# State space preparation of a hybrid trunk: the small response products of two quads issued together, their results side by side in the scratch

## The chip, the cores and the metric

The kernel runs on one core of a Trainium2 chip. The metric is the device time of one execution in microseconds (us). Before the change it is 2791.68 us, the median of 3 runs (2790.18 to 2793.75). One execution was also taken by the hardware profiler; its own time and its trace are what the sections below read.

## The reference

The program is a decoder trunk of two layers over 256 tokens with width 2048. Each layer is a token mixer, a cross-attention to 256 memory positions and a squared-ReLU MLP, each behind an RMSNorm, with residual adds. Layer 0 mixes tokens with a chunked gMLP, layer 1 with a state space layer (S5). All is float32. The change touches only what prepares layer 1's state space layer. Its reference is, cut to what matters:

```python
def s5_glu(h, w_in, lam_re, lam_im, log_dt, bm_re, bm_im, cm_re, cm_im, d_skip, w_out, b_out):
    u = (h @ w_in).reshape(bsz, seq, 128, 16)             # 128 channel groups of 16
    lam_bar = jnp.exp(lam * dt)                            # 128 x 64 complex poles
    b_bar = ((lam_bar - 1.0) / lam)[..., None] * bmat      # 128 x 64 x 16
    bu = jnp.einsum('gpc,bsgc->sbgp', b_bar, u)
    states[s] = lam_bar * states[s - 1] + bu[s]            # an associative scan over positions
    y = jnp.einsum('gcp,sbgp->bsgc', cmat, states).real + d_skip * u
    val, gate = jnp.split(gelu(y) @ w_out + b_out, 2, axis=-1)
    return val * jax.nn.sigmoid(gate)
```

The kernel cuts the 256 positions into 32 chunks of T = 8. Inside a chunk, y is a causal convolution: the response at distance w is the real 16 x 16 matrix C lam_bar^w B_bar of each group, for w = 0 to 7, and D is added at w = 0. These matrices depend on parameters alone. Computing them is the work that the change edits.

## The kernel before, in words

**Weight streams.** Nearly the whole kernel is a stream of matrix products with weights read once. A load of 512 KB (`wraw`, issued by SyncE at L123, four buffers) is split into a high part by ScalarE (`whi`, L102) and a rest by VectorE (`wlo`, L103), three buffers of each. A split load is called a weight tile here. TensorE then runs 12 or 16 matmuls on it: high part by activation high and low part, and rest by activation high part. In the MLP, up-projection tiles are lines L167 (512 wide) and L172 (256 wide), down-projection tiles are L806, L807 and L809 (512 wide). The MLP's hidden activations pass from the accumulator over ScalarE (`r`, L183), VectorE (L184, L641) and a split of their own (`hh` L102, `hl` L103).

**The preparation.** `ssm_prep` appends small steps to a list of side work. It is worked off during layer 0's MLP: `tick` is called after each weight tile, and at every second call one step is recorded at lower priority (a lag of 200). A scheduler of the framework then fixes the order of each engine's instructions at build time; on the chip each engine runs its own list in that order and waits by semaphores.

The 128 groups are treated in 32 quads of four. For each quad q there are three steps:

- `quad(q)` builds `bb`, the B_bar of four groups (L1069 to L1071, VectorE, 128 x 64). There are two `bb` buffers, used in turn; each group's 16 columns are padded to 32 with zeros.
- `quad_q(q)` builds `qt`, the C lam_bar^w (L1079 to L1081, VectorE, 128 x 576 each, two buffers), sends it to the DRAM scratch `Qd`, then multiplies: four matmuls (L1092), one for each group, 32 stationary columns, 128 moving columns, each to its own 32 partitions of one PSUM tile `kp`. In the trace each of these is two instructions, and stands under the tile name `ps`. The responses go from PSUM to `kd`: zeros in the first 7 of 15 blocks (POOL memset, L1095), w = 1 to 7 by a ScalarE copy (L1096), w = 0 with D by VectorE (L1097). Four transfers (L1100, GpSimd queue) write `kd` to the scratch `Kd`, 240 runs of 64 bytes each.
- `quad_p(q)` builds and sends `Pd` (L1110 to L1114).

**The use.** `s5` reads the scratch back on the GpSimd queue (L1144: `pq`, `dq`, `qq`). `own` (L1207) and `outputs` (L1255, L1261) multiply with it in groups of small matmuls; L1207 and L1255 have the same form as L1092, 32 stationary and 128 moving columns, the one 64 and the other 16 instructions in a row.

## Time and profile before

| | |
|---|---|
| median of 3 runs | 2791.68 us (2790.18 to 2793.75) |
| the profiled execution, its own time | 2790.06 us |
| its span, first to last instruction | 2788.4 us |
| TensorE matmul busy | 2765.7 us, 99% |
| VectorE, ScalarE, GpSimd busy | 1986.2, 1395.3, 236.0 us |
| granted TensorE clock, mean | 0.999 |
| the 32 groups of response products (L1092) | 256 instructions, from 779.3 to 1321.5 us |

PE is TensorE's matmuls, PEld its weight loads, DVE VectorE, ACT ScalarE, POOL GpSimd, SP SyncE. Matmuls are pipelined: the recorded duration of one (390 ns for 512 columns) overlaps the next, so what one costs in a stream is the distance from its start to the next start. A row of the timeline gives start, length, engine, line, tiles, shape and count, and in brackets the idle time of the engine ahead of it.

### The profile page before, as it was taken

What the parts mean: (1) busy time and instruction counts of PE and PEld (TensorE: products, weight loads), DVE (VectorE), ACT (ScalarE), POOL (GpSimd) and SP (SyncE); (2) the same over time, 40 slices, a digit from 0 to 9 for tenths busy, and PEclk for the clock granted to TensorE, in tenths of its full rate; (3) what the DMA queues carried; (4) which work ended last, traced back from release to release, by engine and by line L of the source; (5) the groups of instructions that cost most, each with busy time, mean ns of one, the idle gap of its engine ahead of it and who ended that gap; (6) DMA issues with size and microseconds to landing.
All of it is one profiled execution on the core that took longest, in us unless ns stands there. A gap on an engine that the chain in (4) does not pass through costs nothing. (4 is left out here: it accounts for less than half of the span.)

```text
span 2788.4 us, 39687 instructions
## 1 busy us (share of the span) xinstructions
PE 2765.7 (99%) x15020; PEld 2331.1 (84%) x15020; DVE 1986.2 (71%) x2747; ACT 1395.3 (50%) x1801; POOL 236.0 (8%) x434
## 2 busy tenths in 40 slices
PE   9999999999999999999999999999999999999998
PEld 7888888888888888888887888888888888888886
DVE  6765756778978878787568657557777767677665
ACT  6545545555534444444555445445555545455454
POOL 0100000001022222231213100000000000000000
PEclk9999999999999999999999999999999999999999
DMA  8766655547688888887879767564556566565655
GB/s 294 226 216 216 204 177 179 177 156 250 212 261 258 258 257 259 259 257 224 244 244 266 218 199 238 173 196 159 177 156 219 168 217 198 166 218 171 218 180 156
DMA packets 196048, 593.76 MB, mean 213 GB/s; under 512 B 44960, under 2 KB 47184, under 8 KB 195344
## 3 DMA queue, kind: packets, MB, share of 16 engines
q1 hardware_dynamic: 151968, 532.22, 60.6%
q0 software_dynamic: 43744, 58.95, 7.7%
q8 instruction: 117, 1.92, 0.3%
q14 instruction: 75, 0.61, 0.1%
q10 hardware_dynamic: 144, 0.07, 0.0%
HBM read 567.51 MB, written 23.46 MB: 212 GB/s over the span
## 5 line engine op out<-in xcount | busy, mean ns | idle before, releaser
L103 DVE TENSOR_TENSOR wlo<-wraw,whi 128x1024 fp32r<-128x1024 f32 x892 | 1085.1, 1222 | 490.0 <-ACT whi L102 484.3
L102 ACT CAST whi<-wraw 128x1024 fp32r<-128x1024 f32 x892 | 936.9, 1052 | 853.5 <-PE acc L723 202.8
L167 PE MATMUL acc<-act,whi 128*128 128x512 f32 x3072 | 742.3, 391 | 0.9 <-ACT whi L102 0.9
L167 PEld LDWEIGHTS acc<-act,whi 128*128 128x128 f32 x3072 | 562.8, 188 | 111.7 <-issue 2.6
L172 PEld LDWEIGHTS acc<-act,wlo 128*128 128x128 f32 x3072 | 394.9, 191 | 17.6 <-DVE wlo L103 1.9
L172 PE MATMUL acc<-act,wlo 128*128 128x256 f32 x3072 | 403.6, 283 | 1.4 <-DVE wlo L103 1.0
L152 PE MATMUL acc<-whi,act 128*128 128x512 f32 x1472 | 369.7, 393 | 7.1 <-ACT whi L102 6.3
L152 PEld LDWEIGHTS acc<-whi,act 128*128 128x128 f32 x1472 | 274.9, 189 | 64.9 <-ACT whi L102 6.3
L723 PE MATMUL acc<-whi,act 128*128 128x512 f32 x864 | 232.9, 392 | 0.0
L807 PE MATMUL acc<-whi,hl 128*128 128x512 f32 x544 | 213.3, 392 | 0.0
L806 PE MATMUL acc<-whi,hh 128*128 128x512 f32 x544 | 212.7, 391 | 0.0
L152 PE MATMUL acc<-wlo,act 128*128 128x512 f32 x736 | 197.1, 389 | 0.0
L723 PEld LDWEIGHTS acc<-whi,act 128*128 128x128 f32 x864 | 160.4, 188 | 36.5 <-ACT ends L755 1.9
L152 PEld LDWEIGHTS acc<-wlo,act 128*128 128x128 f32 x736 | 138.2, 188 | 28.9 <-DVE wlo L103 0.2
L723 PE MATMUL acc<-whi,hh 128*128 128x512 f32 x378 | 148.4, 393 | 0.0
L723 PE MATMUL acc<-whi,hl 128*128 128x512 f32 x378 | 147.2, 390 | 0.0
L809 PE MATMUL acc<-wlo,hh 128*128 128x512 f32 x544 | 145.9, 390 | 0.0
L723 PE MATMUL acc<-wlo,act 128*128 128x512 f32 x432 | 133.1, 390 | 0.0
L807 PEld LDWEIGHTS acc<-whi,hl 128*128 128x128 f32 x544 | 102.1, 188 | 23.0 <-issue 2.2
L183 ACT COPY r<-acc 128x512 f32<-128x512 f32 x64 | 37.7, 588 | 166.6 <-PE acc L167 166.6
L809 PEld LDWEIGHTS acc<-wlo,hh 128*128 128x128 f32 x544 | 102.1, 188 | 21.5 <-issue 0.2
L806 PEld LDWEIGHTS acc<-whi,hh 128*128 128x128 f32 x544 | 102.1, 188 | 21.4 <-issue 0.4
(365 smaller groups left out, 2763.7 us busy)
## 6 DMA issues: line engine op xcount, KB each, us to landing
wraw<-in_f_w_up SPq DMA_DIRECT2D x256, 512.0 KB, 4.6
wraw<-in_f_w_down SPq DMA_DIRECT2D x228, 512.0 KB, 4.6
wraw<-in_a_w_in SPq DMA_DIRECT2D x64, 512.0 KB, 4.7
wraw<-in_x_w_q SPq DMA_DIRECT2D x64, 512.0 KB, 3.9
wraw<-in_x_w_k SPq DMA_DIRECT2D x64, 512.0 KB, 4.6
wraw<-in_b_w_out SPq DMA_DIRECT2D x64, 512.0 KB, 4.4
wraw<-in_x_w_v SPq DMA_DIRECT2D x48, 512.0 KB, 3.9
wraw<-in_x_w_o SPq DMA_DIRECT2D x48, 512.0 KB, 4.3
```

What stands on the lines that cost most here:

```text
L102: self.nc.scalar.copy(out=hi, in_=src)
L103: return self.nc.vector.tensor_tensor(out=lo, in0=src, in1=hi.bitcast(F32), op=ALU.subtract).ins
L152: nc.tensor.matmul(out[t], a[:, kt, sl], b[:, kk, :], start=st and a is ah, stop=en)
L167: nc.tensor.matmul(acc[:, f, :], hi[:, kk, sl], both[:, kt].rearrange("p a s -> p (a s)"), start=first and kk == 0, stop=last and kk == FK ...
L172: nc.tensor.matmul(acc[:, f, 0:S], lo[:, kk, sl], ah[:, kt, :], start=False, stop=last and kk == FK - 1, skip_group_check=True)
L183: nc.scalar.copy(out=dst, in_=acc[:, :, S:])
L723: mm = lambda s, m, e: nc.tensor.matmul(out, s, m, start=key not in begun, stop=e, skip_group_check=True)
L806: nc.tensor.matmul(acc[:, t, :], ah, hi[:, kk, :], start=kt == 0, stop=False)
L807: nc.tensor.matmul(acc[:, t, :], al, hi[:, kk, :], start=False, stop=False)
L809: nc.tensor.matmul(acc[:, t, :], hid[kt // 4][0][:, kt % 4, sl], lo[:, kk, :], start=False, stop=kt == KT - 1)
```

## The change

The products of two quads (2m and 2m + 1, a pair) are issued together, at the end of the odd quad's `quad_q`, by a new function `products(m)`: eight matmuls into one PSUM tile. One ScalarE copy of twice the size moves w = 1 to 7 of both, and two VectorE instructions add D. `kd` holds both quads side by side in one buffer instead of two; its zeros are written once, in `poles`. Four transfers a pair write it, 240 runs of 128 bytes each, where eight wrote runs of 64 bytes. The scratch's order of axes changes with it, and with that the order in which `outputs` reads `dq`.

```diff
-        self.Kd = mk("Kd", [16, NL, 2, 4, 16])
+        self.Kd = mk("Kd", [16, NL, 4, 2, 16])
...
+            e["kd"] = pool.tile([P, NL, 2, 16], F32, name="kd", bufs=1)
+            nc.gpsimd.memset(e["kd"][:, 0:T - 1], 0.0)
...
             nc.gpsimd.dma_start(out=self.Qd[q // 2][q % 2].rearrange("p r n -> r p n"), in_=qt[:, 1:])
-            kp = self.ps([P, T, 16])
-            for g in range(4):
-                with self.tc.high_priority(offset=g):
-                    nc.tensor.matmul(kp[32 * g:32 * g + 32], bb[:, g], qt[:, 0:T, g, :], start=True, stop=True,
-                                     skip_group_check=True)
-            kd = pool.tile([P, NL, 16], F32, name="kd", bufs=2)
-            nc.gpsimd.memset(kd[:, 0:T - 1, :], 0.0)
-            nc.scalar.copy(out=kd[:, T:, :], in_=kp[:, 1:, :])
-            v.scalar_tensor_tensor(out=kd[:, T - 1, :], in0=eye, scalar=dsk[:, q:q + 1], in1=kp[:, 0, :],
-                                   op0=ALU.mult, op1=ALU.add)
+            e["qt", q] = qt
+            if q % 2:
+                products(q // 2)
+
+        def products(m):
+
+            kp = self.ps([P, 2, T, 16])
+            for i in range(2):
+                bb, qt = e["bb"][i], e.pop(("qt", 2 * m + i))
+                for g in range(4):
+                    with self.tc.high_priority(offset=4 * i + g):
+                        nc.tensor.matmul(kp[32 * g:32 * g + 32, i], bb[:, g], qt[:, 0:T, g, :], start=True, stop=True,
+                                         skip_group_check=True)
+            kd = e["kd"]
+            nc.scalar.copy(out=kd[:, T:].rearrange("p w i c -> p i w c"), in_=kp[:, :, 1:, :])
+            for i in range(2):
+                q = 2 * m + i
+                v.scalar_tensor_tensor(out=kd[:, T - 1, i, :], in0=eye, scalar=dsk[:, q:q + 1], in1=kp[:, i, 0, :],
+                                       op0=ALU.mult, op1=ALU.add)
             for t in range(4):
-                nc.gpsimd.dma_start(out=self.Kd[q // 2][:, :, q % 2, t], in_=kd[32 * t:32 * t + 16])
+                nc.gpsimd.dma_start(out=self.Kd[m][:, :, t], in_=kd[32 * t:32 * t + 16])
...
-                    dq = ahead.pop(("dq", n, i)).rearrange("p (j l t c) -> p l t j c", j=T, l=2, t=4)
+                    dq = ahead.pop(("dq", n, i)).rearrange("p (j t l c) -> p l t j c", j=T, l=2, t=4)
```

Line numbers grow by two from `quad` on and by eleven behind `products`; the products are L1102 in the new file, the copy L1106, the addition of D L1108, the transfers L1111.

The order of instructions changes at two places that matter below. The first is TensorE's list in the up-projection of layer 0's MLP, where the products of the fifth and sixth quad stand (`bb_5745` and `bb_5746` are the two `bb` buffers). Before:

```order
L167 MATMUL acc<-act,whi 128x512 x2
L1092 MATMUL ps<-qt,bb_5745 32x128 x4
L167 MATMUL acc<-act,whi 128x512 x14
L172 MATMUL acc<-act,wlo 128x256 x16
L167 MATMUL acc<-act,whi 128x512 x16
L172 MATMUL acc<-act,wlo 128x256 x16
L167 MATMUL acc<-act,whi 128x512 x8
L1092 MATMUL ps<-qt,bb_5746 32x128 x4
L167 MATMUL acc<-act,whi 128x512 x8
```

The same stretch of TensorE's list in the change:

```order
L172 MATMUL acc<-act,wlo 128x256 x16
L167 MATMUL acc<-act,whi 128x512 x16
L172 MATMUL acc<-act,wlo 128x256 x16
L167 MATMUL acc<-act,whi 128x512 x8
L1102 MATMUL ps<-qt,bb_5745 32x128 x4
L1102 MATMUL ps<-qt,bb_5746 32x128 x4
L167 MATMUL acc<-act,whi 128x512 x8
```

The even quad's four matmuls left their place and stand directly ahead of the odd quad's, which stay where they were. All 32 quads do the same: 16 places instead of 32. TensorE's list is otherwise the same from end to end.

The second is VectorE's list behind the products of the fourth quad (the second of a pair). Before, it reads, from the addition of D to the next rest of a weight tile:

```order
L1097 SCALAR_TENSOR_TENSOR kd<-eye,dsk,ps 128x16
L1069 TENSOR_TENSOR bb_5746<-F,bcq 128x4x16
L1079 TENSOR_TENSOR qt<-T_5684,bcq 128x4x9x16
L1071 TENSOR_TENSOR bb_5746<-bb_5746,tq 128x4x16
L1062 TENSOR_SCALAR bcq<-bcq,sg 128x128
L1080 TENSOR_TENSOR tq<-T_5685,bcq 128x576
L1081 TENSOR_TENSOR qt<-qt,tq 128x4x9x16
L1111 TENSOR_TENSOR tq<-lb 128x512
L103 TENSOR_TENSOR wlo<-wraw,whi 128x1024
```

In the change, from the addition of D for the same pair:

```order
L1108 SCALAR_TENSOR_TENSOR kd<-eye,dsk,ps 128x16 x2
L1071 TENSOR_TENSOR bb_5745<-F,bcq 128x4x16
L1081 TENSOR_TENSOR qt<-T_5684,bcq 128x4x9x16
L1073 TENSOR_TENSOR bb_5745<-bb_5745,tq 128x4x16
L1071 TENSOR_TENSOR bb_5746<-F,bcq 128x4x16
L1082 TENSOR_TENSOR tq<-T_5685,bcq 128x576
L1081 TENSOR_TENSOR qt<-T_5684,bcq 128x4x9x16
L1083 TENSOR_TENSOR qt<-qt,tq 128x4x9x16
L103 TENSOR_TENSOR wlo<-wraw,whi 128x1024
```

Before, one quad (the sixth, `bb_5746`) starts to build its `bb` and `qt` here, and the fifth had started six weight tiles earlier. Now both quads of the next pair start here, since both buffers of each come free together, and L1111 and L1062 stand elsewhere.

## The prediction

> **What bounds the kernel now.** I read the page first, then the stretch in which the edited work runs (740 to 1340 us), then who waits there. From the page, the windows view (after the window: its length, then busy time of PE, PEld, DVE, ACT and POOL, granted clock, DMA share, GB/s), and the waits of that stretch (who waited for whom: us in total, times, longest):

> ```profile
> span 2788.4 us, 39687 instructions
> PE 2765.7 (99%) x15020; PEld 2331.1 (84%) x15020; DVE 1986.2 (71%) x2747; ACT 1395.3 (50%) x1801; POOL 236.0 (8%) x434
> ...
> 740.00:1340.00 600.00, 600.00 (x3203) 499.84 (x3202) 476.91 (x712) 260.94 (x309) 149.56 (x274) 1.00 0.84 254
> 1340.00:1580.00 240.00, 237.51 (x1999) 191.45 (x1997) 160.03 (x310) 129.58 (x216) 49.28 (x85) 1.00 0.83 241
> ...
> ACT whi L102 <- PE acc L807: 154.2, 102, 1.7
> POOL kd L1095 <- DMA Kd<-kd: 64.0, 28, 4.2
> DVE bb L1069 <- PE ps L1092: 17.0, 13, 1.8
> ```

> PE is busy for all 600.00 us of the stretch (the second window is the state space layer behind it), at a clock of 1.00, and no wait of PE appears in it. Everyone else waits for PE: ScalarE for a weight buffer that PE must free, VectorE for the products. So the stretch lasts as long as PE's list takes to issue. An edit on POOL, ACT, DVE or the DMA queues gains nothing here while PE stays fed; an edit of PE's list counts in full.

> **What a group of products costs.** PE's timeline around the first group; the columns are start, length, engine, line, what, count:

> ```profile
> 776.97 1.07 PE L809 MATMUL acc<-wlo,hh 128*128 128x512 f32 x4
> 779.01 0.39 PE L807 MATMUL acc<-whi,hl 128*128 128x512 f32 x1
> 779.33 0.43 PE L1092 MATMUL ps<-qt,bb 128*32 128x128 f32 x8
> 779.68 0.50 PE L806 MATMUL acc<-whi,hh 128*128 128x512 f32 x1
> 780.02 0.39 PE L807 MATMUL acc<-whi,hl 128*128 128x512 f32 x1
> 780.25 1.09 PE L809 MATMUL acc<-wlo,hh 128*128 128x512 f32 x4
> 782.99 1.07 PE L809 MATMUL acc<-wlo,hh 128*128 128x512 f32 x4
> 785.71 1.07 PE L809 MATMUL acc<-wlo,hh 128*128 128x512 f32 x4
> ```

> A weight tile takes 785.71 - 782.99 = 2.72 us from one L809 to the next. The tile that holds the group takes 780.25 - 776.97 = 3.28, the one behind it still 2.74. The group therefore costs 0.56 + 0.02 = 0.58 us. Only part of that is the eight instructions, which run from 779.33 to 779.68 together with the way out. The rest lies at the borders: the L807 ahead takes 0.32 to the next start instead of 2.72 / 12 = 0.23, and the L806 behind takes 0.34. The 32 groups cost 32 x 0.58 = 18.6 us.

> A pair's group has 16 instructions of the same form. The trace has this form in longer runs, in the state space layer itself:

> ```profile
> 1458.22 0.64 PE L1255 MATMUL ps<-dq,us 128*32 128x128 f32 x16
> 1458.80 0.69 PE L1261 MATMUL ps<-qq,vv 64*32 64x128 f32 x32
> ...
> 1427.28 1.95 PE L1207 MATMUL ps<-pq,us 128*32 128x128 f32 x64
> 1429.16 1.20 PE L152 MATMUL acc<-whi,act 128*128 128x512 f32 x4
> ```

> From first start to the start of what follows: 0.35 us for 8 (L1092), 0.58 for 16 (L1255), 1.88 for 64 (L1207). From 8 to 64 it is (1.88 - 0.35) / 14 = 0.109 us for each further four instructions, and from 8 to 16 0.23 / 2 = 0.115: the borders are paid once however long the run is. The second quad then adds 0.22 us to a group that is open already.

> **The change part by part.** PE, removed: 16 groups, at 0.58 us each 9.3 us. PE, added: 16 x 0.22 = 3.5 us of longer groups. Net 0.36 us a pair, 5.8 us in all. The bounds are the second quad for nothing (9.3 us gained) and the second quad at the full price of a group (nothing gained). I take 5.8, since L1255 and L1207 are the same form and agree within 0.006 us; starts are given to 0.01 us, which leaves 0.34 to 0.38 a pair, 5.4 to 6.1.

> [...]

> The other engines' parts, from the groups of the same stretch (count | busy, mean ns):

> ```profile
> L1096 ACT COPY kd<-ps 128x112 f32<-128x112 f32 x32 | 8.1, 253 | 16.8 <-PE ps L1092 15.5 <-issue 1.2
> L1097 DVE SCALAR_TENSOR_TENSOR kd<-eye,dsk,ps 128x16 f32<-128x16 f32 x32 | 7.2, 225 | 0.0
> L1100 POOL DMA_DIRECT2D Kd<-kd x128 | 73.1, 587 | 289.4 <-issue 268.6 <-DVE kd L1097 20.7
> L1095 POOL MEMSET kd<- 128x112 f32 x30 | 5.7, 190 | 64.2 <-DMA Kd<-kd 64.0
> L1069 DVE TENSOR_TENSOR bb<-F,bcq 128x64 f32<-128x64 f32 x30 | 6.7, 223 | 17.2 <-PE ps L1092 17.0
> L1079 DVE TENSOR_TENSOR qt<-T,bcq 128x576 f32<-128x576 f32 x32 | 24.0, 751 | 0.0
> ```

> POOL loses 64 issues (64 x 0.587 = 37.6 us), 31 memsets (31 x 0.19 = 5.9 us) and the 64 us of waiting ahead of them; the queues lose half of the packets of `Kd`. ACT trades 32 copies of 0.25 us for 16 of twice the width, 4 to 8 us in all. DVE's count stays. All of this lies beside PE's full 600 us, so I cost it at nothing. Without that cover it would be a gain.

> Two waits change. `kd` has one buffer, so a pair's copy on ACT, with the `whi` casts queued behind it, waits for the four transfers of the pair before. The first group starts at 779.3 and the last at 1321.5, so pairs lie some 35 us apart, while the longest that POOL's memset waited for such transfers was 4.2 us; the wait ends long before the copy. And `bb` and `qt` of both quads of the next pair now wait for one group, with VectorE's weight rests queued behind them. What VectorE has in hand there is read from before, behind the fourth quad's group:

> ```profile
> 845.29 1.23 DVE L103 TENSOR_TENSOR wlo<-wraw,whi 128x1024 fp32r<-128x1024 f32 x1 [0.35 <-ACT whi L102]
> 846.43 0.23 DVE L1097 SCALAR_TENSOR_TENSOR kd<-eye,dsk,ps 128x16 f32<-128x16 f32 x1
> 849.29 0.69 DVE L1111 TENSOR_TENSOR tq<-lb 128x512 f32<-128x512 f32 x1
> 849.89 1.22 DVE L103 TENSOR_TENSOR wlo<-wraw,whi 128x1024 fp32r<-128x1024 f32 x1
> 851.40 1.23 DVE L103 TENSOR_TENSOR wlo<-wraw,whi 128x1024 fp32r<-128x1024 f32 x1
> ...
> 850.11 2.08 PE L172 MATMUL acc<-act,wlo 128*128 128x256 f32 x16
> 855.68 0.52 PE L172 MATMUL acc<-act,wlo 128*128 128x256 f32 x3
> ```

> Between two rests stands a string of small work from 846.43 to 849.89, 3.5 us. The two rests made behind it end at 851.1 and 852.6. PE consumes two rests in each run of 16 L172; the run at 850.11 uses those made before the string, and the next, at 855.68, these two: the first has 4.6 us in hand, the second (needed half of the run's 2.08 us later) 4.1. In the new order the string there gains one L1097, one L1069 and one L1079 (0.22 + 0.22 + 0.75) and loses L1111 (0.69) and L1062: the first rest comes at most 0.5 us later, the second, with L1111 now ahead of it, at most 1.2. The 4.1 us cover that, and I cost it at nothing; without the cover it is up to 1.2 us a pair, 19 us.

> The reading side is left alone: `dq` has the same bytes and the same strides in its rows, only the offsets of l and t change places.

> The sum: profiled execution 2790.06 - 5.8 = 2784.3 us. It stood 1.6 us under the median, so for the median 2791.68 - 5.8 = **2785.9 us**, 0.21% less.

> **The rivals.** *A little of it is given back* (2786.2 to 2790). PE loses tenths of a microsecond at some pairs, because a rest or a hidden activation comes late behind the longer string. For it: VectorE is busy 476.9 of 600 us, and the new order packs two quads where one stood. Against it: the 4.1 us in hand. At 0.2 us a pair it is 3.2 us, which gives 2789.1.

> *The borders are not what costs.* If each set of four with its own `bb` pays its own way in and out, the pair costs 2 x 0.58 as before: 2791.7, no change. L1207 and L1255 speak against it, since each of their sets of four loads other weights too and still adds 0.11 us.

> *VectorE becomes late for good* (slower). The second quad's `bb` and `qt`, L1069, L1079 and L1081 (same size, taken at the same 0.75), 0.22 + 0.75 + 0.75 = 1.72 us, move from a place six tiles earlier to one directly ahead of the rests. If PE had nothing in hand there, each pair would wait that long: 16 x 1.72 = 27.5 us, 2791.7 - 5.8 + 27.5 = 2813.4. It decides as soon as the 4.1 us in hand are used up; 0.36 us a pair cancels the gain.

> *Faster loads* are no gain of their own: POOL, the queues and VectorE get relief, but PE has no wait in the stretch that this could shorten.

> **How the numbers follow.** Between runs the kernel differs by 3.6 us (2790.18 to 2793.75), so about 0.2%, 5.6 us, is what a measurement can tell from no change. My 5.8 us lies on that line, and a median that is off by a microsecond puts it on either side. The forecast of 2785.9 gets a chance of 0.70, of which 0.45 comes out beyond 5.6 us and 0.25 short of it; the small loss gets 0.16 and no saving 0.08, both within 0.2%; VectorE late gets 0.06, nearly all of it slower. That makes faster by over 0.2% 0.45, within 0.2% 0.50 and slower 0.05. The range leaves out the last two rivals, takes in the small loss, and on the other side a third of the way from 5.8 to the second quad for nothing (9.3 us) and a microsecond or two of a lucky median: 2782.6 to 2790.6.

> **What would show it.** In the trace after, the products (now L1102) should stand in 16 runs of 16 instructions, each from first start to the next line's start 0.57 us, and the tile that holds one should take some 0.80 us more than the 2.72 between two L809. Windows without a group should read as before, PE should be busy for the whole stretch, and the last product should start some 5.5 us earlier than 1321.5. POOL's wait for `Kd` should be gone without any trace of it in the span. It is wrong if PE shows waits for `wlo` or `hl` behind the groups (VectorE), or if a run of 16 takes 1.1 us (borders within a run). The time alone can be off, with all of this right, through the span outside the stretch, where 2.5 us of PE idle lie in the state space layer.

## The result: 0.14% slower, with TensorE's list as short as forecast

| | before | after |
|---|---|---|
| median, 22 runs each | 2792.78 us (2789.22 to 2796.62) | 2797.15 us (2790.06 to 2804.36) |
| ratio | | 1.0014, 95% interval 1.0008 to 1.0021 |
| profiled execution, its own time | 2790.06 us | 2798.56 us |

The forecast was 2785.9 us, in a range of 2782.6 to 2790.6. The time came out above the range, on the other side of no change, and the runs spread twice as wide as before.

From the page of the kernel after, the busy times:

```profile
PE 2764.4 (99%) x15020; PEld 2333.9 (83%) x15020; DVE 1979.6 (71%) x2747; ACT 1393.0 (50%) x1785; POOL 191.0 (7%) x339
```

Its windows view over the edited stretch; columns as before:

```profile
740.00:1340.00 600.00, 594.95 (x3197) 500.96 (x3197) 470.49 (x715) 258.79 (x292) 104.22 (x177) 1.00 0.82 251
```

PE was busy for 600.00 us of this window before; now 5.05 us are idle. The groups themselves are as forecast. PE's timeline around a pair's group, after:

```profile
906.68 1.77 PE L167 MATMUL acc<-act,whi 128*128 128x512 f32 x7
908.38 0.64 PE L1102 MATMUL ps<-qt,bb 128*32 128x128 f32 x16
908.95 2.14 PE L167 MATMUL acc<-act,whi 128*128 128x512 f32 x8
```

The run of 16 takes 908.95 - 908.38 = 0.57 us to the next start, the figure of the forecast to the hundredth. With the two lists laid side by side matmul by matmul, PE is 0.33 to 0.36 us further ahead behind each of the 16 pairs, some 5.5 us in all.

That is the gain. It is overpaid by waits that the kernel before did not have. The waits of the stretch, 740 to 1345 us (who waited for whom: us in total, times, longest), after:

```profile
DVE po L1121 <- DMA Pd<-po: 30.4, 7, 5.3
DVE po L1121 <- DMA lb<-Ld: 12.5, 3, 6.7
ACT whi L102 <- DMA wraw<-in_f_w_up: 20.8, 12, 4.6
ACT whi L102 <- DMA wraw<-in_f_w_down: 13.4, 6, 4.5
PE acc L172 <- DVE wlo L103: 5.0, 5, 3.0
DVE bb L1071 <- PE ps L1102: 2.9, 4, 1.0
SPq L1056 <- DVE tq L1122: 22.3, 19, 8.9
```

L1121 is the first instruction of `quad_p` (L1110 before). VectorE stands still 42.9 us in front of it, ten times, for two kinds of transfer: for `Pd` to have left the `po` buffer that it writes, and for `lb`, its operand. Before, it waited for neither. ScalarE now waits 34.2 us for weights and PE 5.0 us for weight rests; both are absent in the stretch before. The wait that the forecast looked at, `bb` for the products, shrank from 17.0 to 2.9 us.

### The profile page after: what moved, and what is told of

Read it like the earlier page. It is cut to its first block, busy times and chain, and to the rows that moved or that the text cites. A ratio compares the mean times of both kernels' runs of the same rounds, so it can differ in the third digit from the quotient of the medians.

```text
span 2796.8 us, 39441 instructions
## 1 busy us (share of the span) xinstructions
PE 2764.4 (99%) x15020; PEld 2333.9 (83%) x15020; DVE 1979.6 (71%) x2747; ACT 1393.0 (50%) x1785; POOL 191.0 (7%) x339
## 5 line engine op out<-in xcount | busy, mean ns | idle before, releaser
L103 DVE TENSOR_TENSOR wlo<-wraw,whi 128x1024 fp32r<-128x1024 f32 x892 | 1084.4, 1222 | 479.4 <-ACT whi L102 474.2
L102 ACT CAST whi<-wraw 128x1024 fp32r<-128x1024 f32 x892 | 936.8, 1052 | 861.3 <-PE acc L723 206.2
L172 PEld LDWEIGHTS acc<-act,wlo 128*128 128x128 f32 x3072 | 395.5, 191 | 24.4 <-DVE wlo L103 9.3
L172 PE MATMUL acc<-act,wlo 128*128 128x256 f32 x3072 | 405.3, 284 | 6.6 <-DVE wlo L103 6.2
L152 PE MATMUL acc<-whi,act 128*128 128x512 f32 x1472 | 369.6, 393 | 8.2 <-ACT whi L102 6.6
L152 PEld LDWEIGHTS acc<-whi,act 128*128 128x128 f32 x1472 | 274.7, 189 | 66.5 <-ACT whi L102 6.6
L807 PE MATMUL acc<-whi,hl 128*128 128x512 f32 x544 | 212.7, 391 | 0.0
L806 PE MATMUL acc<-whi,hh 128*128 128x512 f32 x544 | 212.6, 391 | 0.0
L152 PE MATMUL acc<-wlo,act 128*128 128x512 f32 x736 | 197.2, 389 | 0.1
L152 PEld LDWEIGHTS acc<-wlo,act 128*128 128x128 f32 x736 | 138.0, 188 | 29.1 <-DVE wlo L103 0.5
L809 PE MATMUL acc<-wlo,hh 128*128 128x512 f32 x544 | 145.9, 390 | 0.0
L807 PEld LDWEIGHTS acc<-whi,hl 128*128 128x128 f32 x544 | 102.1, 188 | 22.2 <-issue 1.0
L809 PEld LDWEIGHTS acc<-wlo,hh 128*128 128x128 f32 x544 | 102.0, 188 | 21.7 <-DVE wlo L103 0.3
L806 PEld LDWEIGHTS acc<-whi,hh 128*128 128x128 f32 x544 | 102.1, 188 | 21.4 <-issue 0.2
L183 ACT COPY r<-acc 128x512 f32<-128x512 f32 x64 | 37.6, 587 | 163.6 <-PE acc L167 163.6
```

What stands on the lines that cost most here:

```text
L102: self.nc.scalar.copy(out=hi, in_=src)
L103: return self.nc.vector.tensor_tensor(out=lo, in0=src, in1=hi.bitcast(F32), op=ALU.subtract).ins
L152: nc.tensor.matmul(out[t], a[:, kt, sl], b[:, kk, :], start=st and a is ah, stop=en)
L172: nc.tensor.matmul(acc[:, f, 0:S], lo[:, kk, sl], ah[:, kt, :], start=False, stop=last and kk == FK - 1, skip_group_check=True)
L183: nc.scalar.copy(out=dst, in_=acc[:, :, S:])
L806: nc.tensor.matmul(acc[:, t, :], ah, hi[:, kk, :], start=kt == 0, stop=False)
```

## How one such wait reaches TensorE

The third stall is the longest. The timeline around it, after; what stands in brackets is the idle time ahead of an instruction and what ended it:

```profile
1231.51 0.58 SPq L1056 DMA_DIRECT2D lb<-Ld  x1
1236.98 0.75 DVE L1083 TENSOR_TENSOR qt<-qt,tq 128x576 f32<-128x576 f32 x1
1240.07 3.82 PE L167 MATMUL acc<-act,whi 128*128 128x512 f32 x16
1244.43 0.69 DVE L1121 TENSOR_TENSOR po<-lb 128x512 f32<-128x512 f32 x1 [6.71 <-DMA lb<-Ld]
1245.04 0.68 DVE L1122 TENSOR_TENSOR tq<-lb 128x512 f32<-128x512 f32 x1
1245.64 1.22 DVE L103 TENSOR_TENSOR wlo<-wraw,whi 128x1024 fp32r<-128x1024 f32 x1
1246.43 0.59 SPq L1056 DMA_DIRECT2D lb<-Ld  x1
1246.92 1.22 PE L172 MATMUL acc<-act,wlo 128*128 128x256 f32 x8 [3.03 <-DVE wlo L103]
1247.13 5.82 SPq L123 DMA_DIRECT2D wraw<-in_f_w_up  x4
1248.39 1.97 PE L172 MATMUL acc<-act,wlo 128*128 128x256 f32 x8 [0.25 <-DVE wlo L103]
```

Read it downwards. VectorE is done with a `qt` at 1237.7, then stands before L1121 for 6.71 us because its `lb`, issued at 1231.51, lands only 12.8 us later. The profile names the transfer that lands last; the `po` buffer that L1121 writes was free hardly earlier, since its `Pd`, issued at 1231.97, landed at 1243.5. The next weight rest, L103, is behind L1121 in VectorE's list and starts only at 1245.64; PE has its high parts done at 1243.9, and waits 3.03 us for that rest. SyncE's queue is held too: it may load `lb` again only when L1122 has read the buffer (at 1245.04), and the four weight loads of 1247.13 stand behind that.

The two other stalls have a `po` buffer as their cause. The first, with the transfer that holds the buffer, after:

```profile
832.62 0.69 DVE L1121 TENSOR_TENSOR po<-lb 128x512 f32<-128x512 f32 x1 [5.34 <-DMA Pd<-po]
846.56 0.64 PE L1102 MATMUL ps<-qt,bb 128*32 128x128 f32 x16
855.72 0.58 POOL L1125 DMA_DIRECT2D Pd<-po  x1 [2.73 <-DVE bcq L1064]
867.48 0.69 DVE L1121 TENSOR_TENSOR po<-lb 128x512 f32<-128x512 f32 x1 [5.33 <-DMA Pd<-po]
868.09 1.22 DVE L103 TENSOR_TENSOR wlo<-wraw,whi 128x1024 fp32r<-128x1024 f32 x1
869.36 1.22 PE L172 MATMUL acc<-act,wlo 128*128 128x256 f32 x8 [0.66 <-DVE wlo L103]
```

The same quad, before:

```profile
824.09 0.69 DVE L1110 TENSOR_TENSOR po<-lb 128x512 f32<-128x512 f32 x1
838.49 0.56 POOL L1114 DMA_DIRECT2D Pd<-po  x1 [0.35 <-DVE wlo L103]
860.06 0.68 DVE L1110 TENSOR_TENSOR po<-lb 128x512 f32<-128x512 f32 x1
```

L1121 opens a `po` early, since it needs nothing but `lb` and a free buffer. The rest of `quad_p` works in the same `tq` as the quad's own `qt`, and comes only behind that. Before, the buffer opened at 824.09 was sent at 838.49, 14.4 us later, and was wanted again at 860.06: 21.6 us for a transfer that landed after 9.6 in the median. After, the buffer opened at 832.62 was sent at 855.72, 23.1 us later. The `qt` of this quad had to wait for the pair's group at 846.56, as the other quad's did. The buffer's next use follows 11.8 us behind the transfer's issue, as late as the transfer lands. The quad shown held its buffer long before the change too: over all 32 quads the median from opening to sending is 7.1 us before and 21.3 us after.

So the quads come in twos. Before, a quad's first instruction (L1069) started every 12 to 17 us (813, 830, 847, 859, 872, 889); after, two start together every 27 to 35 us (814 and 816, 849 and 850, 876 and 878, 909 and 911). `po` and `lb` have two buffers each, and what was spread over a pair's time now wants both at once, and then a third.

## The experiments

The two theories. **Bunching:** the gain of 5.8 us is real, and it is lost because both quads of a pair hold their buffers until one late group frees them; VectorE then waits at L1121 for transfers. **The string:** VectorE's list behind the group is simply too long, or the new scratch costs time by itself. Unless said otherwise each kernel is the change with one edit.

Besides medians I use a second measure, which leaves out what varies elsewhere in the program: the start of the same matmul in the profiled execution of a kernel and in the one of the kernel before, at 740 and at 1335 us. What the delay grows by between the two is the loss within the stretch, in one execution each.

| kernel | ratio to before, 95% | median | delay at 740 | at 1335 | in the stretch |
|---|---|---|---|---|---|
| the change | 1.0014 (1.0008 to 1.0021) | 2797.15 us | 2.3 | 5.1 | +2.8 us |
| early_pairs | 0.9978 (0.9969 to 0.9987) | 2787.91 | 2.7 | -2.4 | -5.1 |
| spread_products | 1.0004 (0.9995 to 1.0013) | 2794.09 | 1.8 | 2.5 | +0.7 |
| split_products | 1.0000 (0.9991 to 1.0009) | 2793.21 | 3.3 | 3.3 | 0.0 |
| pairs_old_scratch | 1.0062 (1.0048 to 1.0075) | 2808.14 | 0.5 | 18.9 | +18.3 |
| no_fifth | 1.0056 (1.0044 to 1.0069) | 2807.70 | 4.1 | 17.2 | +13.1 |
| four_po | 1.0032 (1.0020 to 1.0044) | 2802.00 | 4.9 | 11.9 | +6.9 |
| three_lb | 1.0014 (1.0006 to 1.0023) | 2796.41 | 3.3 | 4.0 | +0.7 |

The first four experiments shared runs of the kernel before with a median of 2792.71 us, the last three with one of 2792.74.

### The group, issued as soon as the odd quad is ready

The 16 matmuls keep together, but get a high priority, so that the scheduler puts them where the odd quad's `qt` is done and not six weight tiles later. In its trace the two `bb` of a pair still start together (807, 839, 875), but L1121 starts every 17 us or so (828, 845, 862, 879), and VectorE's list has it directly ahead of the two instructions that finish its `po`.

```diff
-            for i in range(2):
+            for i in (1, 0):
                 bb, qt = e["bb"][i], e.pop(("qt", 2 * m + i))
                 for g in range(4):
-                    with self.tc.high_priority(offset=4 * i + g):
-                        nc.tensor.matmul(...)
+                    with self.tc.high_priority(offset=1000 + g), (nullcontext() if i else self.tc.issue_after(mm)):
+                        mm = nc.tensor.matmul(...).ins
```

> The change, with one thing altered: the pair's eight products get a high priority and the odd quad's four stand ahead of the even quad's, so that they are issued as soon as the odd quad's qt is ready and not about six weight tiles (17 us) later. Still 16 groups of 16 instructions. By the order both bb buffers still come free together, but the two quads' other work on VectorE is 5 to 7 weight tiles apart again. Theory A (the pairs' late products make two quads start together; VectorE then reaches L1121 before po's transfer or lb's load is done, the weight rests queue behind it and PE runs dry): no wait of L1121 on a DMA, no PE wait for wlo in 740 to 1340 us, time before minus 5.5, about 2787. Theory B (the single kd buffer, the double copy or the new layout of the scratch costs the time): all of that is still in, so about 2797, as the change.

Measured: 2787.91 us, ratio 0.9978 (0.9969 to 0.9987). It is faster than the kernel before and than the change. Windows and waits of the stretch:

```profile
740.00:1340.00 600.00, 599.62 (x3232) 506.18 (x3231) 482.12 (x720) 262.17 (x295) 112.62 (x190) 1.00 0.86 259
PE ps L1102 <- DVE qt L1083: 0.3, 1, 0.3
```

No wait of L1121 for a transfer is left in this stretch, nor one of PE for a rest. And its `po`, in the timeline:

```profile
862.36 0.68 DVE L1121 TENSOR_TENSOR po<-lb 128x512 f32<-128x512 f32 x1
863.42 0.42 DVE L1124 TENSOR_TENSOR po<-po,tq 128x256 f32<-128x256 f32 x1
864.14 0.55 POOL L1125 DMA_DIRECT2D Pd<-po  x1 [9.64 <-DVE po L1124]
```

From opening the buffer to its transfer it takes 1.8 us, where it was 14.4 before and 23.1 in the change; the median of the 32 quads is 1.8 us. The even distance of the quads and L1121's new place in VectorE's list come together here and are not told apart. What follows: grouping pays, and the place of the group decides whether the payment is kept.

### The same early place, without the groups

The high priority alone, with the matmuls in the order of the change: the scheduler then leaves each quad's four at a place of their own, 32 places.

```diff
-                    with self.tc.high_priority(offset=4 * i + g):
+                    with self.tc.high_priority(offset=1000 + 4 * i + g):
```

> The change with a high priority of the products but without holding the even quad's back: PE issues each quad's four as soon as its qt is ready, in 32 places; all of the rest of the change stays. Theory A: no waits of L1121, and no gain of the groups either: 2792.8 within 2 us, so 5.5 us over early_pairs, which prices the grouping alone. Theory B: 2797 to 2802.

Measured: 2794.09 us, ratio 1.0004 (0.9995 to 1.0013). Beside early_pairs this is the price of the borders, taken by time: 2794.09 - 2787.91 = 6.2 us for 16 pairs, where the forecast had 5.8. It also shows that the early place is worth nothing by itself that can be measured.

### The new scratch alone

Each quad's four matmuls stay where they were before; one PSUM tile, one `kd`, four transfers a pair, the zeros written once, and the order of axes are those of the change.

```diff
-            e["qt", q] = qt
+            if q % 2 == 0:
+                e["kp"] = self.ps([P, 2, T, 16])
+            kp, i = e["kp"], q % 2
+            for g in range(4):
+                with self.tc.high_priority(offset=g):
+                    nc.tensor.matmul(kp[32 * g:32 * g + 32, i], bb[:, g], qt[:, 0:T, g, :], ...)
             if q % 2:
                 products(q // 2)
...
```

> The change without the grouping on PE: each quad's four products are issued at their old place into their half of the pair's PSUM tile; the single copy, the single kd with zeros set once, the four transfers a pair and the layout stay. Theory A: quads are spaced as before the change, no DMA wait of L1121, 32 groups of 0.58 us; time as before, 2792.8 within 2 us. Theory B: 2797 or more, since everything but the grouping's gain remains (by B 2797 + 5.5 = 2802).

Measured: 2793.21 us, ratio 1.0000 (0.9991 to 1.0009). Windows and waits of the stretch:

```profile
740.00:1340.00 600.00, 600.00 (x3210) 500.14 (x3209) 476.74 (x720) 259.20 (x294) 105.66 (x178) 1.00 0.84 252
DVE bb L1071 <- PE ps L1096: 17.2, 13, 1.8
```

PE is full again, L1121 waits for no transfer, and VectorE's wait for the products is that of the kernel before, 17.0 us there. Half of the `Kd` issues, gone from a stretch in which PE is fed, are worth nothing that can be measured; nor does the new scratch do harm. So the loss comes in with the pairing of the matmuls.

### The pairs with the old scratch

The other half: groups of 16 as in the change, but two `kd` buffers, a memset for each, eight transfers of 64-byte runs, the old axes.

```diff
-            nc.scalar.copy(out=kd[:, T:].rearrange("p w i c -> p i w c"), in_=kp[:, :, 1:, :])
             for i in range(2):
+                kd = pool.tile([P, NL, 16], F32, name="kd", bufs=2)
+                nc.gpsimd.memset(kd[:, 0:T - 1, :], 0.0)
+                nc.scalar.copy(out=kd[:, T:, :], in_=kp[:, i, 1:, :])
...
+                for t in range(4):
+                    nc.gpsimd.dma_start(out=self.Kd[m][:, :, i, t], in_=kd[32 * t:32 * t + 16])
```

> The change's grouping on PE alone: products of two quads together, but kd per quad in two buffers, zeros set each time, two copies and eight transfers a pair with the old layout of the scratch. Theory A: the quads start together as in the change, so L1121 (here a few lines further) waits for Pd and lb by about 40 us in all and PE runs dry at a few places; time as the change, about 2797 (2793 to 2802). Theory B: with the old scratch side the time falls to before minus 5.5, about 2787.

Measured: 2808.14 us, ratio 1.0062 (1.0048 to 1.0075), above what I had expected. Windows and waits of the stretch:

```profile
740.00:1340.00 600.00, 584.59 (x3109) 491.38 (x3111) 460.83 (x699) 251.48 (x293) 133.58 (x243) 0.99 0.80 246
DVE po L1120 <- DMA Pd<-po: 46.9, 9, 8.6
PE acc L172 <- DVE wlo L103: 7.9, 4, 3.1
PE acc L809 <- DVE wlo L103: 7.5, 3, 2.8
```

The direction is that of the bunching: the pairing alone, without the scratch, is the harmful half. The size was a surprise: 18.3 us are lost in the stretch where the change loses 2.8, and the wait for `Pd` grows from 30.4 to 46.9 us. One part is the clock. In this execution the granted clock is halved for 3.4 us at four places of the stretch (near 1008, 1046, 1186 and 1223 us; its mean over the 600 us is 0.99), in that of the change at one (near 1249; 1.00). At half pace each place costs about 1.7 us, half of the 3.4, an estimate by which the three more make 5 of the 15.5 us between the two. Why `Pd` frees its `po` later stays open: GpSimd issues it 0.7 us behind the start of its last writer in both kernels, and it lands 10.5 us after that issue against 9.7 in the change (all medians). By the medians of the runs the leaner scratch does gain in the change, 2808.14 - 2797.15 = 11 us, though alone it gained nothing.

### More buffers for what is waited for

The room for another `po` or `lb` is taken from the fifth weight buffer of this MLP, 4 KB a partition. The control gives that buffer up; the two others spend its room, one on four `po` of 2 KB instead of two, one on three `lb` of 4 KB. (The `pw` of earlier steps shares the buffers of `lb` and gets the third one too.) The lists of PE, VectorE, ScalarE and POOL are the same in all three and in the change.

```diff
-            self.fifth = None if nxt.closing else mp
+            self.fifth = None
```

> The change without the fifth load buffer (every fifth weight load of layer 0's MLP has one of its own): a control for the two kernels beside it, which need its 4 KB. A buffer less ahead makes weights late behind the stalls sooner: 2797 to 2805. The waits of L1121 as in the change, some 40 us in all.

```diff
-            po = pool.tile([P, 4, 2, 64], F32, name="po", bufs=2)
+            po = pool.tile([P, 4, 2, 64], F32, name="po", bufs=4)
```

> The change with four po buffers instead of two, in the room of the fifth load buffer. If po's transfers are what VectorE waits for, the waits of L1121 on Pd are gone and those on lb stay or grow (about 12 to 25 us); PE runs dry at fewer places: 4 to 8 us under no_fifth. If instead the pairs' string of small work on VectorE is too long by itself, the time is that of no_fifth within 2 us.

```diff
-                e["lb", q] = pool.tile([P, 2, 4, 2, 64], F32, name="lb", bufs=2)
+                e["lb", q] = pool.tile([P, 2, 4, 2, 64], F32, name="lb", bufs=3)
```

> The change with three lb buffers instead of two, in the room of the fifth load buffer: loads of lb no longer wait for the quad before the last. L1121's waits on lb (12.5 us of the change's 43) go, those on Pd (30.4 us) stay or grow: 0 to 3 us under no_fifth, less than four_po.

Measured: 2807.70, 2802.00 and 2796.41 us. The control lies above what I had expected: giving up the fifth weight buffer costs 10.6 us by itself. The waits of the stretch, of the control first:

```profile
DVE po L1121 <- DMA Pd<-po: 19.6, 4, 5.7
DVE po L1121 <- DMA lb<-Ld: 19.5, 4, 6.7
PE acc L172 <- DVE wlo L103: 9.0, 11, 2.5
SPq L1056 <- DVE tq L1122: 22.1, 18, 9.0
```

With four `po`:

```profile
DVE po L1121 <- DMA lb<-Ld: 26.0, 8, 6.9
PE acc L172 <- DVE wlo L103: 4.9, 5, 3.1
```

With three `lb`:

```profile
DVE po L1121 <- DMA Pd<-po: 34.2, 7, 6.3
PE acc L172 <- DVE wlo L103: 3.9, 5, 2.0
SPq L1056 <- DVE tq L1122: 0.2, 1, 0.2
```

Each addition takes away its own wait altogether, part of which moves to the other, and with the same work in the same order the time falls, by 5.7 us for `po` and by 11.3 for `lb`. So too few buffers are a cause of the loss, not a sign of it. For `po` the way is the wait of L1121, which falls from 39.1 to 26.0 us in all while SyncE's wait ahead of the loads of `lb` stays at 22 us. With five and six runs the intervals of the two kernels just meet.

For `lb` it is in part another. That this addition is the larger one was not expected, and L1121's wait is hardly the whole reason, since it falls by 5 us only, from 39.1 to 34.2. What also goes with the third buffer is SyncE's wait ahead of the loads of `lb`, behind which weight loads stand: ScalarE waits 76.0 us for weights, where it waits 103.6 in the control and 99.3 with four `po`. How much of the 11.3 us each of the two waits makes is not separated. Both additions at once were not run.

## Why the prediction was wrong, by its own steps

**PE's list bounds the stretch: right, as a condition.** It held while PE was fed, in the kernel before and in split_products (600.00 of 600 us) and in early_pairs (599.62). The edit itself ended it.

**A pair saves 0.36 us, 5.8 in all: right.** 0.33 to 0.36 a pair in the traces, 6.2 us by time with the group at an early place. The rival that the borders are not what costs falls.

**POOL's relief at nothing: right where PE is fed** (split_products), wrong beside the pairing, where the new scratch as a whole, POOL's relief with it, is worth 11 us. I had costed it with the cover of PE's full 600 us, and the same change took that cover away.

**The wait for the single `kd`: right.** ScalarE's copy L1105 shows no wait for a `Kd` transfer, only 6.7 us for the products.

**VectorE: the step that failed.** I wrote "The 4.1 us cover that, and I cost it at nothing". I had counted by how much VectorE's string behind a group grows, and behind the groups PE indeed shows no wait. I had not asked what the two quads that start together hold, and who asks for it next. L1110, which becomes L1121, stands in neither of the strings that I compared, and I did not follow it: it asks for a `po` whose transfer was issued 11.8 us ago, or for an `lb` whose load has not landed. A wait there is up to 6.7 us, beyond the 4.1 in hand, and the rests stand behind it. So the term that I put at nothing was ten such waits, 42.9 us on VectorE, of which three stalls reached PE and cost 8.3 us.

The sum with that step measured, for the profiled execution of the change: 16 pairs gain 5.5 us. Three stalls, at 868, 1209 and 1244, cost 2.0, 0.8 and 5.5, 8.3 together, of which the last has 3.3 us of idle and 2.2 behind it, most of them from matmuls at half the clock (below). So the stretch up to 1335 ends 8.3 - 5.5 = 2.8 us later. The rest of the 8.5 us between the two profiled executions lies outside: 2.3 us ahead of 740, and 3.3 behind 1335, 2.3 of them in the state space layer. The medians differ by 4.4 us only, and other kernels here show 0.5 to 4.9 us ahead of 740, where nothing was edited, so I don't put these down to the change. What the new axes of `dq` may cost in the state space layer is within the interval of split_products, some 2.5 us either way; closer than that it stays open.

**The rivals.** *VectorE becomes late for good* had the right engine and the right sign, with a chance of 0.06, but by another mechanism and not at each pair: its 1.72 us a pair and 27.5 in all were the length of the string. What was missing was a rival of transfers: buffers in twos, quads in twos. The sign that I had named for being wrong, PE waiting for `wlo`, is the one that came, though 21 to 28 us behind a group and not right behind it, as I had it.

## What to carry to other kernels

When work is merged so that two users give their buffers back at once, follow each buffer that they hold from its first writer to the landing of its transfer, and compare that time with the distance to its next writer; the instruction that waits there holds everything behind it in its engine's list, as L1121 held L103 here for 6.71 us. The saved border costs on the engine that sets the time were real here (6.2 us for 16 pairs), but put the merged group where its last input is ready, not where the later half happened to stand. And an edit that is worth nothing beside a fed TensorE (the scratch, ratio 1.0000) may be worth several microseconds (11 here) once another part of the same change starves it.

## What the runs showed of the hardware that was not expected

```profile
1185.13 1.36 PE L809 MATMUL acc<-wlo,hh 128*128 128x512 f32 x4 [2.01 <-DVE wlo L103]
1186.30 0.63 PE L806 MATMUL acc<-whi,hh 128*128 128x512 f32 x1
1186.72 0.63 PE L807 MATMUL acc<-whi,hl 128*128 128x512 f32 x1
...
1186.00:1189.30 3.30, 3.30 (x10) 2.53 (x9) 3.30 (x7) 0.20 (x1) 0.56 (x1) 0.50 0.92 275
```

Behind a wait of 2.01 us, starts lie 0.42 us apart instead of 0.23, from about 1186 to 1189.4; the granted clock is 0.50 there, and by 1190.50 the starts lie 0.23 apart again. In the change the same stands behind 1248.39, after waits of 3.03 and 0.25 us: eight L172 in 1.97 us, where the eight ahead of them had 1.22. The granted clock is 1.00 from 1247 to 1248, 0.50 from 1249 to 1251 and 1.00 again from 1252 to 1253.

Whether it happens is not a matter of the waits' length alone. Of the state space layer, where no kernel edits them, the same eight matmuls behind the same two waits (1.20 us, shortly ahead of what is shown, and 0.79), in the kernel before:

```profile
1510.59 2.11 PE L152 MATMUL acc<-whi,act 128*128 128x512 f32 x8 [0.79 <-ACT u L1182]
1510.50:1513.90 3.40, 3.31 (x15) 2.75 (x16) 3.37 (x6) 2.17 (x4) 3.10 (x6) 1.00 0.77 209
```

and in early_pairs (1.23 and 0.79):

```profile
1508.21 3.61 PE L152 MATMUL acc<-whi,act 128*128 128x512 f32 x8 [0.79 <-ACT u L1193]
1508.20:1511.50 3.30, 3.29 (x8) 2.62 (x9) 3.27 (x6) 1.05 (x2) 1.87 (x5) 0.50 1.10 270
```

These are 1.5 us more at half the clock; what decides between the two is not shown. This may be one reason why single executions here differ by a few microseconds, and one why the runs of the change, which has more such waits (PE idle for 5.05 us of the stretch, against none), spread wider; in its runs the mean granted clock lies between 0.996 (2801.44 us) and 0.999 (2790.06 us).
